# A chunked recurrence whose ten-step inverse is spread over two rounds instead of one

## The chip, the core and the metric

The kernel runs on one core of a Trainium2 chip. The metric is the device time of one execution in microseconds. The core has five engines, each of which executes its own instructions in their order and waits for others by semaphores: TensorE (PE, matrix products, output to the PSUM memory), VectorE (DVE) and ScalarE (ACT, both elementwise), GpSimd (POOL) and SyncE (SP, which here issues the DMA transfers).

## The reference

Two layers over 512 latent and 256 context tokens of width 1024. Each layer mixes tokens by attention and by a gated recurrence (RWKV-7), projects, and then runs a product-key expert layer (PEER). Only the recurrence is touched. Per head (8 heads of 64, two directions) it is a scan over the tokens:

```python
def step(state, inp):
    r_t, w_t, k_t, v_t, kk_t, b_t = inp
    s_kk = jnp.einsum('bhij,bhj->bhi', state, kk_t)
    state = state * w_t[:, :, None, :] - s_kk[..., None] * b_t[:, :, None, :] + v_t[..., None] * k_t[:, :, None, :]
    y = jnp.einsum('bhij,bhj->bhi', state, r_t) if emit else None
    return state, y
...
for d in range(N_DIRS):
    reverse = d == 1
    s_ctx, y_ctx = rwkv_direction(feats_ctx, d, s0, reverse, need_ctx_out)
    _, y_lat = rwkv_direction(feats_lat, d, s_ctx, reverse, True)
```

The latent scan starts from the state in which the context scan ended. In the last layer the context outputs are not wanted.

## The kernel before

The function `rwkv` runs once per layer. It cuts the scan into 12 chunks of 64 tokens, 4 of context and 8 of latents, with all 8 heads and both directions of a chunk side by side in one set of tiles. Inside a chunk the steps are done as matrix products, which needs the inverse of a 64 by 64 triangular matrix for each head and direction. Only the state `H` passes from chunk to chunk. The work on a chunk is cut into stages; each is a list of small functions:

- `load`: twelve DMAs, all issued by SP, bring the chunk's features: eight into `fal` (L755), four into `fbl` (L757). Both tiles have two buffers, so the load for a chunk waits until the chunk two before it has been read.
- stage_a: `Ex` and `En`, exponentials of the decays, on ScalarE (L768, L769), from `fbl`; then on VectorE `etot`, `KR` (L777, L779), `bh` and `kh` (L783, L784), and on ScalarE `vz`.
- stage_b: products of `KR` with `bh` and `kh`. `dm` (L797) is the first of their results on VectorE, followed by `AT`, `BG`, `GK` (L804 to L813); then transposed copies `kn`, `BG`, `Vb` on ScalarE.
- stage_c: the inverse of the 8 by 8 blocks on the diagonal, some thirty small VectorE instructions (D8 L837, Nb L843, the X chain L848 to L852) up to the first `W` (L856).
- stage_d: ten steps that make the whole inverse of it, each needing the one before: three times [`WT`: transpose on TensorE (the flip, L736) and copy on ScalarE (L740); `S`: product W·AT on TensorE and subtraction on VectorE (L873); `W`: product S·WT and copy on ScalarE (L879)], and last `XB`: product BG·W and copy on ScalarE (L886).
- stage_e: with the state of the chunk before, `Zs` (L910), the new `H` (L926 to L929) and the outputs (`Yc`, `Yl`, L947 to L949). `outputs` normalises and gates finished pairs of chunks (L983 to L1015).

The loop at the end of `rwkv` weaves the stages of neighbouring chunks into rounds. In round m stand stage_e of chunk m-2, all of stage_d of chunk m-1, stage_b and stage_c of chunk m, stage_a of chunk m+1, the load of chunk m+2 and the outputs of chunk m-3. `merge` sorts the functions by the positions given (from 0 to 1 within a round); after it a scheduler fixes the order on each engine, which the program then keeps. Products go to a pool of three PSUM buffers, named `wk`. All products of a round are on TensorE in one order (L717, L730, L736 are the helpers that issue them).

Of the kernel before, what the change touches and what calls it, by code (L numbers as in the profile page):

```python
# [101 lines left out]
def body(ctx: ExitStack, tc: tile.TileContext, I: dict, out: bass.AP):  # L102
# [588 lines left out]
    def rwkv(L, PT, cat, FD, need_ctx, ro, rl):  # L691
# [15 lines left out]
        def t8(nm, n, w=64):  # L707
            return ra.tile([128, 4, 2, w], F32, name=nm, bufs=n).rearrange("p g s n -> p s g n")
# [37 lines left out]
        def stage_a(s):  # L746
            def load():
                NCH, n = TOK[s["st"]] // C, s["n"]
                fal = s["fal"] = rl.tile([128, 3, 2, 4, C], F32, name="fal", bufs=2)
                fbl = s["fbl"] = rl.tile([128, 3, 2, 4, C], F32, name="fbl", bufs=2)  # L750
                for hf in range(2):
                    fd = FD[s["st"], hf]
                    for pp in range(2):
                        for d in range(2):
                            SP.dma_start(fal[:, :, pp, 2 * hf + d, :],  # L755
                                         fd["a"][NCH - 1 - n if d else n, pp].rearrange("p (f t) -> p f t", t=C))
                        SP.dma_start(fbl[:, :, pp, 2 * hf:2 * hf + 2, :],  # L757
                                     fd["b"][n, pp].rearrange("p (f d t) -> p f d t", d=2, t=C))

            def dv(f, d):  # L760
                t = s["fal"][:, f, :, d::2, :]
                return t[:, :, :, ::-1] if d else t

            def a1():
                Ex = s["Ex"] = t8("Ex", 2, 65)
                En = s["En"] = t8("En", 2)
                V.memset(Ex[:, :, :, 0:1], 1.0)
                A.activation(Ex[:, :, :, 1:65], s["fbl"][:, 2], AF.Exp, scale=-EXPC)  # L768
                A.activation(En, s["fbl"][:, 2], AF.Exp, scale=EXPC)  # L769
                s["etot"] = t8("etot", 5, 1)  # L770
                V.tensor_copy(s["etot"], Ex[:, :, :, 64:65])

            def a2(d):
                if d == 0:
                    s["KR"] = t8("KR", 4, 128)
                KR, Ex = s["KR"], s["Ex"]
                V.tensor_tensor(KR[:, :, d::2, 0:64], dv(1, d), Ex[:, :, d::2, 0:64], op=mul)  # L777
                if s["emit"]:
                    V.tensor_tensor(KR[:, :, d::2, 64:128], dv(0, d), Ex[:, :, d::2, 1:65], op=mul)  # L779

            def a3():
                s["kh"], s["bh"], s["vz"] = t8("kh", 2), t8("bh", 2), t8("vz", 2)
                V.tensor_tensor(s["bh"], s["fbl"][:, 1], s["En"], op=mul)  # L783
                V.tensor_tensor(s["kh"], s["fbl"][:, 0], s["En"], op=mul)  # L784
                for d in range(2):
                    A.copy(s["vz"][:, :, d::2, :], dv(2, d))

            return [load], [a1, lambda: a2(0), lambda: a2(1), a3]

        def stage_b(s):  # L790
            w = 128 if s["emit"] else 64

            def b0():
                gt = quad(work(), 64)
                cross(gt, s["KR"][:, :, :, 0:64], s["bh"])
                dm = s["dm"] = t8("dm", 1)
                V.tensor_tensor(dm, gt, bc(K("n8")), op=mul)  # L797

            def b1():
                gb = quad(work(), w)  # L800
                cross(gb, s["bh"], s["KR"][:, :, :, :w])
                s["AT"] = t8("AT", 3)
                BG = s["BG"] = t8("BG", 3, 128)
                V.tensor_tensor(s["AT"], gb[:, :, :, 0:64], bc(K("mp")), op=mul)  # L804
                if s["emit"]:
                    V.tensor_tensor(BG[:, :, :, 64:128], gb[:, :, :, 64:128], bc(K("n")[:, 64:128]), op=mul)
                V.tensor_tensor(s["AT"], s["AT"], bc(K("eye")), op=add)

            def b2():
                gk = quad(work(), w)  # L810
                cross(gk, s["kh"], s["KR"][:, :, :, :w])
                s["GK"] = t8("GK", 3, 128)
                V.tensor_tensor(s["GK"][:, :, :, :w], gk,  # L813
                                K("m")[:, None, None, :w].to_broadcast([128, 2, 4, w]), op=mul)

            def b3():
                t = work()
                flips(t[:, 0, :], s["kh"])
                flips(t[:, 1, :], s["bh"])
                s["kn"] = t8("kn", 3)  # L820
                unflip(s["kn"], t[:, 0, :])
                unflip(s["BG"][:, :, :, 0:64], t[:, 1, :], -0.5)

            def b4():
                t = work()
                flips(t[:, 0, :], s["vz"])
                s["Vb"] = t8("Vb", 3)
                unflip(s["Vb"], t[:, 0, :])

            return [b0, b1, b2, b3, b4]  # L830

        def stage_c(s):
            w = {}

            def c0():
                w["D"] = ra.tile([128, 8, 8], F32, name="D8", bufs=2)
                V.tensor_reduce(w["D"], flat(s["dm"]).rearrange("p x (b j) -> p x j b", j=8), axis=AX.X, op=add)  # L837

            def c2(q0):
                if q0 == 1:  # L840
                    w["N"] = ra.tile([128, 8, 8, 8], F32, name="Nb")
                for q in range(q0, min(8, q0 + 4)):
                    V.stream_shuffle(w["N"][:, q], w["D"], [(x // 8) * 8 + q for x in range(32)])  # L843

            def c3(q):
                if q == 7:
                    w["X"] = ra.tile([128, 8, 8], F32, name="X8", bufs=2)
                    V.tensor_copy(w["X"], K("eye8")[:, None, :].to_broadcast([128, 8, 8]))  # L848
                tm = ra.tile([128, 8, 8], F32, name="xtm", bufs=2)
                X8, Nb = w["X"], w["N"]  # L850
                V.tensor_tensor(tm[:, :, :q], X8[:, :, q:q + 1].to_broadcast([128, 8, q]), Nb[:, q, :, :q], op=mul)
                V.tensor_tensor(X8[:, :, :q], X8[:, :, :q], tm[:, :, :q], op=add)  # L852

            def c4():
                W = s["W"] = t8("W", 4)
                V.tensor_tensor(flat(W).rearrange("p x (b t) -> p x b t", t=8),  # L856
                                w["X"][:, :, None, :].to_broadcast([128, 8, 8, 8]),
                                K("x8")[:, None, :, None].to_broadcast([128, 8, 8, 8]), op=mul)

            return [c0, lambda: c2(1), lambda: c2(5)] + [lambda q=q: c3(q) for q in range(7, 0, -1)] + [c4]  # L860

        def stage_d(s):
            def d0():
                t = work()
                flips(t[:, 0, :], s["W"])
                s["WT"] = t8("WT", 2)
                unflip(s["WT"], t[:, 0, :])

            def d1():
                t = quad(work(), 64)  # L870
                cross(t, s["AT"], s["W"])
                s["S"] = t8("S", 2)
                V.tensor_tensor(s["S"], bc(K("eye2")), t, op=sub)  # L873

            def d2():
                t = quad(work(), 64)
                cross(t, s["WT"], s["S"])
                s["W"] = t8("W", 4)
                A.copy(s["W"], t)  # L879

            def d3():
                w = 128 if s["emit"] else 64
                t = quad(work(), w)
                cross(t, s["W"], s["BG"][:, :, :, :w])
                s["XB"] = t8("XB", 2, 128)
                A.copy(s["XB"][:, :, :, :w], t)  # L886

            return [d0, d1, d2] * 3 + [d3]
# [137 lines left out]
        NI = len(items)  # L1026
        for f in AA[0][0] + AA[0][1] + AA[1][0]:
            f()
        for st in ("c", "l")[0 if need_ctx else 1:]:
            gate_in(st)  # L1030
        for m in range(NI + 2):
            todo = []
            if m >= 2:
                todo.append((0.0, 0.8, stage_e(SS[m - 2])))
            if 1 <= m <= NI:
                todo.append((0.02, 1.0, stage_d(SS[m - 1])))
            if m < NI:
                todo.append((0.0, 0.4, stage_b(SS[m])))
                todo.append((0.15, 1.0, stage_c(SS[m])))
            if m >= 3:  # L1040
                st, n = items[m - 3]
                if (st == "l" or need_ctx) and n >= TOK[st] // C // 2:
                    todo.append((0.0, 0.9, outputs(st, n, bank)))
            if m + 2 < NI:
                todo.append((0.0, 0.1, AA[m + 2][0]))
            if m + 1 < NI:
                todo.append((0.55, 1.0, AA[m + 1][1]))
            merge(*todo)
# [729 lines left out]
```

## Time and profile before

| | us |
|---|---|
| median of 3 runs (lowest, highest) | 4801.51 (4800.45, 4802.5) |
| profiled execution, own time | 4804.7 |
| its span, first to last instruction | 4802.9 |
| TensorE busy, share of the span | 4308.1, 90% |
| VectorE busy | 3620.7, 75% |
| ScalarE busy | 1942.4, 40% |
| mean granted TensorE clock | 0.953 |

The span is taken by the hardware profiler and is 1.8 us shorter than that execution's time. Times of instructions are counted from the span's start. The recurrence of layer 0 runs from about 463 to 778 us, that of layer 1 from about 3125 to 3418 us. Shares over the whole span say little of them: most of it is the projections and the expert layers.

### The profile page before, as it was taken

Reading aid. Unit: us, or ns where it says so; the run is one execution under the profiler, and the core shown is the slowest. Engines: PE = TensorE matmul, PEld = TensorE weight load, DVE = VectorE, ACT = ScalarE, POOL = GpSimd, SP = SyncE. Lnnn points to the kernel's source line nnn. Section 1 sums busy time; section 2 is a strip of 40 time slices with the busy share of each in tenths; the row PEclk is TensorE's granted clock in tenths of the full one; section 3 lists DMA queues with packets and bytes.
Section 4 is the critical chain, followed back from the end, with each engine's and each line's share of the span. In section 5 each row is a group of like instructions: output and inputs, shape, how many; then the busy total and the mean of one; then the engine's idle time right before and its main releaser. Section 6 shows DMA issues by size and latency. Waiting matters only on the chain. (4 is left out here: it accounts for less than half of the span.)

```text
span 4802.9 us, 85326 instructions
## 1 busy us (share of the span) xinstructions
PE 4308.1 (90%) x32715; PEld 3589.6 (75%) x32715; DVE 3620.7 (75%) x7842; ACT 1942.4 (40%) x3407; POOL 1353.9 (28%) x1256
## 2 busy tenths in 40 slices
PE   7998688886999999988899989867898999999999
PEld 5664576765787887767787778456777997899998
DVE  3457665899997888877788656766579977878885
ACT  3355333435675222222222234633336763333332
POOL 0201001442222345545455231200122102244441
PEclk8999899998999999999999999979999999999999
DMA  6656314535678999988889632751334769999995
GB/s 239 243 174 197 79 51 151 184 118 180 233 267 315 349 323 332 321 292 301 294 324 321 225 126 80 207 133 43 106 132 168 257 237 334 346 330 337 331 329 208
DMA packets 576904, 1106.71 MB, mean 230 GB/s; under 512 B 145328, under 2 KB 358000, under 8 KB 566768
## 3 DMA queue, kind: packets, MB, share of 16 engines
q1 hardware_dynamic: 465904, 698.56, 42.6%
q0 software_dynamic: 110592, 402.70, 23.4%
q8 instruction: 257, 4.21, 0.4%
q14 instruction: 151, 1.24, 0.1%
HBM read 960.37 MB, written 140.74 MB: 229 GB/s over the span
## 5 line engine op out<-in xcount | busy, mean ns | idle before, releaser
L158 PE MATMUL u_ps<-phi,uhi 128*128 128x512 f32 (+1 forms) x2048 | 766.7, 374 | 62.3 <-ACT ga L1473 45.5
L1282 POOL DMA_INDIRECT u<-in_u,eidx x384 | 480.6, 1252 | 1171.6 <-DVE u L1294 833.9
L158 PE MATMUL u_ps<-phi,ulo 128*128 128x512 f32 (+1 forms) x2048 | 757.8, 370 | 35.7 <-DVE ulo L1468 35.5
L158 PE MATMUL u_ps<-plo,uhi 128*128 128x512 f32 (+1 forms) x2048 | 754.8, 369 | 0.0
L1282 POOL DMA_INDIRECT u<-in_v,eidx x384 | 516.1, 1344 | 516.9 <-DVE gacc L1307 437.1
L1467 ACT CAST uhi<-raw 128x1024 fp32r<-128x1024 f32 x256 | 268.4, 1049 | 910.7 <-PE u_ps L158 564.5
L158 PE MATMUL pa<-vhi,whi 128*128 128x512 f32 x1536 | 601.4, 392 | 9.8 <-ACT whi L149 9.8
L158 PE MATMUL pa<-vlo,whi 128*128 128x512 f32 x1536 | 601.0, 391 | 0.0
L158 PE MATMUL pa<-vhi,wlo 128*128 128x512 f32 x1536 | 600.5, 391 | 0.0
L1294 DVE SCALAR_TENSOR_TENSOR u<-u,gh 128x1024 f32<-128x1024 f32 x384 | 469.0, 1231 | 122.7 <-DMA u<-in_u,eidx 113.5
L1307 DVE SCALAR_TENSOR_TENSOR gacc<-u,gw,gacc 128x1024 f32<-128x1024 f32 x381 | 488.2, 1281 | 92.6 <-DMA u<-in_v,eidx 89.4
L158 PEld LDWEIGHTS u_ps<-phi,uhi 128*128 128x128 f32 x2048 | 392.7, 192 | 117.3 <-ACT ga L1473 55.3
L158 PEld LDWEIGHTS u_ps<-phi,ulo 128*128 128x128 f32 x2048 | 392.1, 191 | 83.2 <-DVE ulo L1468 40.5
L158 PEld LDWEIGHTS u_ps<-plo,uhi 128*128 128x128 f32 x2048 | 392.9, 192 | 44.5
L1468 DVE TENSOR_TENSOR ulo<-raw,uhi 128x1024 fp32r<-128x1024 f32 x256 | 312.9, 1222 | 136.3 <-ACT uhi L1467 134.5
L149 ACT CAST whi<-w 128x512 fp32r<-128x512 f32 (+1 forms) x256 | 145.1, 567 | 629.5 <-DVE w L1615 383.3
L158 PEld LDWEIGHTS pa<-vhi,whi 128*128 128x128 f32 x1536 | 290.2, 189 | 69.0 <-issue 10.1
L158 PEld LDWEIGHTS pa<-vhi,wlo 128*128 128x128 f32 x1536 | 289.8, 189 | 61.5
L158 PEld LDWEIGHTS pa<-vlo,whi 128*128 128x128 f32 x1536 | 290.1, 189 | 58.6
L1601 DVE TENSOR_TENSOR vlo<-vraw,vhi 128x1024 fp32r<-128x1024 f32 x256 | 312.2, 1220 | 25.8 <-ACT vhi L1600 25.7
L1600 ACT CAST vhi<-vraw 128x1024 fp32r<-128x1024 f32 x256 | 263.5, 1048 | 57.7 <-PE pa L158 35.2
L1552 DVE TENSOR_SCALAR oh<-cst,gT 128x128 f32<-128x128 f32 x896 | 253.2, 351 | 0.0
(867 smaller groups left out, 8619.1 us busy)
## 6 DMA issues: line engine op xcount, KB each, us to landing
raw<-in_ut SPq DMA_DIRECT2D x256, 512.0 KB
vraw<-in_v SPq DMA_DIRECT2D x256, 512.0 KB
gscr<-Gs SPq DMA_DIRECT2D x28, 2048.0 KB
mod_w<-in_mod_w SPq DMA_DIRECT2D x48, 1024.0 KB
Gt<-gscr SPq DMA_DIRECT2D x32, 1024.0 KB
raw<-in_w_q SPq DMA_DIRECT2D x48, 512.0 KB
Gt<-gscr SPq DMA_DIRECT2D x32, 768.0 KB
wo<-in_w_out SPq DMA_DIRECT2D x40, 512.0 KB
```

The lines of the kernel that those rows point to most:

```text
L149: A.copy(hi, src)
L158: PE.matmul(ps, a, b, start=first and q == 0 and j == 0, stop=last and q == n - 1 and j == 2)
L1282: G.indirect_dma_start(out=t, out_offset=None, in_=I[f"{tab}{l}"], in_offset=bass.IndirectOffsetOnAxis(ap=res["e"][:, e:e + 1], axis=0))
L1294: V.scalar_tensor_tensor(u, u, 1.0, c["h"], op0=mul, op1=mul, accum_out=c["act"][:, e:e + 1])
L1307: V.scalar_tensor_tensor(acc, v, w[:, e:e + 1], acc, op0=mul, op1=add)
L1467: A.copy(uhi, ut)
L1468: ins = V.tensor_tensor(ulo, ut, uhi.bitcast(F32), op=sub)
L1552: V.tensor_scalar(o2[:, t, :], io, T3[:, 1, t0 + t:t0 + t + 1], T3[:, 2, t0 + t:t0 + t + 1], op0=ALU.is_equal, op1=mul)
L1600: A.copy(r["vhi"], vt)
L1601: gafter(V.tensor_tensor(r["vlo"], vt, r["vhi"].bitcast(F32), op=sub), f)
```

## The change

The ten steps of stage_d are cut in two lists of five: `DD[m - 1][:5]` (WT, S, W, WT, S) of a chunk runs in the round in which all ten ran before; `DD[m - 2][5:]` (W, WT, S, W, XB) runs a round later, beside the first five of the next chunk. stage_e and the outputs come one round later too, so the loop has one round more. Tiles that now live longer get more buffers (etot 6, KR 5, AT, BG, GK, kn and Vb 4, W 6). stage_b is spread over 0.6 of a round instead of 0.4. The number of instructions that compute is the same. The edits of `GK`, `kn`, `Vb` and the second `W` have the form of those shown.

```diff
@@ -767,12 +767,12 @@
...
-                s["etot"] = t8("etot", 5, 1)
+                s["etot"] = t8("etot", 6, 1)
...
-                    s["KR"] = t8("KR", 4, 128)
+                    s["KR"] = t8("KR", 5, 128)
...
@@ -799,8 +799,8 @@
...
-                s["AT"] = t8("AT", 3)
-                BG = s["BG"] = t8("BG", 3, 128)
+                s["AT"] = t8("AT", 4)
+                BG = s["BG"] = t8("BG", 4, 128)
...
@@ -852,7 +852,7 @@
...
-                W = s["W"] = t8("W", 4)
+                W = s["W"] = t8("W", 6)
...
@@ -1028,17 +1028,20 @@
             f()
         for st in ("c", "l")[0 if need_ctx else 1:]:
             gate_in(st)
-        for m in range(NI + 2):
+        DD = [stage_d(s) for s in SS]
+        for m in range(NI + 3):
             todo = []
-            if m >= 2:
-                todo.append((0.0, 0.8, stage_e(SS[m - 2])))
+            if m >= 3:
+                todo.append((0.0, 0.9, stage_e(SS[m - 3])))
+            if 2 <= m < NI + 2:
+                todo.append((0.02, 1.0, DD[m - 2][5:]))
             if 1 <= m <= NI:
-                todo.append((0.02, 1.0, stage_d(SS[m - 1])))
+                todo.append((0.1, 1.0, DD[m - 1][:5]))
             if m < NI:
-                todo.append((0.0, 0.4, stage_b(SS[m])))
+                todo.append((0.0, 0.6, stage_b(SS[m])))
                 todo.append((0.15, 1.0, stage_c(SS[m])))
-            if m >= 3:
-                st, n = items[m - 3]
+            if m >= 4:
+                st, n = items[m - 4]
                 if (st == "l" or need_ctx) and n >= TOK[st] // C // 2:
                     todo.append((0.0, 0.9, outputs(st, n, bank)))
             if m + 2 < NI:
```

On ScalarE, in the round of layer 0 that ends at `dm` of chunk 5, this stands around `Ex` of chunk 8 before (names are tiles and their numbers, `out<-in`):

```order
L722 COPY settle_6017<-wk_6000 128x8
L768 ACTIVATE Ex_7447<-fbl_6688 128x2x4x64
L769 ACTIVATE En_7448<-fbl_6688 128x2x4x64
L879 COPY W_6063<-wk_6046 128x2x4x64
L740 ACTIVATE WT_6102<-wk_6097 128x512
L879 COPY W_6169<-wk_6152 128x2x4x64
L886 COPY XB_6198<-wk_6181 128x2x4x128
```

and this after the change:

```order
L786 COPY vz_6413<-fal_5568 128x2x2x64 x2
L879 COPY W_5855<-wk_5838 128x2x4x64
L768 ACTIVATE Ex_7208<-fbl_6421 128x2x4x64
L769 ACTIVATE En_7209<-fbl_6421 128x2x4x64
L879 COPY W_5906<-wk_5889 128x2x4x64
L740 ACTIVATE WT_5919<-wk_5914 128x512
L947 COPY Yc_5497<-zy_5601 128x2x2x64 x2
L886 COPY XB_5964<-wk_5947 128x2x4x128
```

Before, the two `W` copies, a `WT` and the `XB` behind `Ex` all belong to one chunk. After, the `W` copy ahead of `Ex` and the `WT` belong to one chunk, the `W` and the `XB` behind it to the chunk before that.

On TensorE, the same round, up to the product `bh`·`KR` from which `dm` is made, before (cst with W is the flip):

```order
L730 MATMUL zy_5816<-XB_5772,Zs_5945 64x64 x13
L736 MATMUL wk_6097<-cst_60,W_6063 128x128 x4
L717 MATMUL wk_6128<-W_6063,AT_5442 64x64 x16
L717 MATMUL zy_6242<-GK_5485,Vb_5565 64x64 x13
L717 MATMUL wk_6152<-S_6145,WT_6102 64x64 x16
L717 MATMUL zy_6242<-GK_5485,Vb_5565 64x64 x3
L717 MATMUL zy_6242<-Vb_5565,GK_5485 64x64 x8
L717 MATMUL wk_6181<-BG_5443,W_6169 64x128 x16
L717 MATMUL wk_6202<-bh_6175,KR_6104 64x64 x16
```

and after:

```order
L717 MATMUL wk_5889<-S_5829,WT_5749 64x64 x16
L736 MATMUL wk_5914<-cst_60,W_5855 128x128 x4
L730 MATMUL zy_5601<-XB_5538,Zs_5723 64x64 x16
L717 MATMUL wk_5947<-BG_4945,W_5906 64x128 x16
L717 MATMUL wk_5966<-W_5855,AT_5278 64x64 x16
L717 MATMUL wk_6008<-bh_5986,KR_5908 64x64 x16
```

The flip (of W_5855) and the state's products (zy from XB and Zs) now stand ahead of the product BG·W, the steps S·WT and W·AT between them are gone.

On SyncE, a load in layer 1 (chunk 7), before:

```order
L757 DMA fbl_30589<-fdb1l1_26020 128x3x128
L757 DMA fbl_30965<-fdb1l0_26018 128x3x128 x2
L757 DMA fbl_30965<-fdb1l1_26020 128x3x128
L755 DMA fal_30964<-fda1l0_26017 128x3x64 x4
L755 DMA fal_30964<-fda1l1_26019 128x3x64 x4
L757 DMA fbl_30965<-fdb1l1_26020 128x3x128
```

and after:

```order
L757 DMA fbl_30788<-fdb1l0_26018 128x3x128 x2
L757 DMA fbl_30788<-fdb1l1_26020 128x3x128 x2
L755 DMA fal_30787<-fda1l0_26017 128x3x64 x4
L755 DMA fal_30787<-fda1l1_26019 128x3x64 x4
L757 DMA fbl_31164<-fdb1l0_26018 128x3x128 x2
```

The fourth `fbl` transfer has moved from behind the eight `fal` transfers to the front. (The first row of before is of chunk 6, the last of after of chunk 8.)

On VectorE, at the start of layer 0, `bh` and `kh` of chunk 3 stood behind `etot` and the first `KR` of chunk 4, and so behind its `Ex`; after the change they stand ahead of them.

## Rows read from the trace of the kernel before

**Rows 1.** The page, chain that ended last: share of the span by engine

```profile
PE 22%; DVE 2%; DMA 0%; issue 0%; ACT 0%; POOL 0%; DVEq 0%; SPq 0%
```

**Rows 2.** Busy time by stretch: length, each engine, granted clock, DMA share, GB/s

```profile
562.67:589.31 26.64, 18.61 (x569) 16.68 (x569) 15.71 (x51) 8.36 (x18) 0.00 (x0) 0.87 0.25 62
709.83:728.02 18.19, 16.19 (x569) 14.64 (x569) 12.94 (x43) 6.76 (x14) 0.00 (x0) 1.00 0.02 4
577.00:582.40 5.40, 0.08 (x2) 0.00 (x0) 1.50 (x5) 1.62 (x3) 0.00 (x0) 0.89 0.73 183
582.40:588.00 5.60, 5.45 (x128) 4.77 (x132) 1.49 (x3) 1.18 (x2) 0.00 (x0) 0.50 0.33 74
```

**Rows 3.** VectorE in order of time, dm: start, duration, idle before and releaser

```profile
537.05 0.69 DVE L797 TENSOR_TENSOR dm<-wk,cst 128x512 f32<-128x512 f32 x1 [8.88 <-PE wk L717]
...
562.67 0.69 DVE L797 TENSOR_TENSOR dm<-wk,cst 128x512 f32<-128x512 f32 x1 [2.77 <-PE wk L717]
...
589.31 0.69 DVE L797 TENSOR_TENSOR dm<-wk,cst 128x512 f32<-128x512 f32 x1 [3.12 <-PE wk L717]
...
670.98 0.69 DVE L797 TENSOR_TENSOR dm<-wk,cst 128x512 f32<-128x512 f32 x1 [3.35 <-PE wk L717]
...
728.02 0.69 DVE L797 TENSOR_TENSOR dm<-wk,cst 128x512 f32<-128x512 f32 x1 [2.57 <-PE wk L717]
...
3188.88 0.69 DVE L797 TENSOR_TENSOR dm<-wk,cst 128x512 f32<-128x512 f32 x1 [6.18 <-PE wk L717]
...
3210.93 0.69 DVE L797 TENSOR_TENSOR dm<-wk,cst 128x512 f32<-128x512 f32 x1 [5.41 <-PE wk L717]
...
3310.83 0.69 DVE L797 TENSOR_TENSOR dm<-wk,cst 128x512 f32<-128x512 f32 x1 [2.78 <-PE wk L717]
...
3367.70 0.69 DVE L797 TENSOR_TENSOR dm<-wk,cst 128x512 f32<-128x512 f32 x1 [2.57 <-PE wk L717]
```

**Rows 4.** End of the VectorE block at 574 us, and the load behind it

```profile
574.01 0.68 DVE L783 TENSOR_TENSOR bh<-fbl,En 128x512 f32<-128x512 f32 x1
...
574.73 3.55 SPq L757 DMA_DIRECT2D fbl<-fdb0l  x4
```

**Rows 5.** ScalarE in the round from 562.67

```profile
580.75 0.63 ACT L768 ACTIVATE Ex<-fbl 128x512 f32<-128x512 f32 x1 [7.48 <-DMA fbl<-fdb0l]
...
581.81 0.57 ACT L879 COPY W<-wk 128x512 f32<-128x512 f32 x1
```

**Rows 6.** TensorE in the same round

```profile
582.43 1.11 PE L736 MATMUL wk<-cst,W 128*128 128x128 f32 x4 [5.35 <-ACT W L879]
...
587.34 1.43 PE L717 MATMUL wk<-BG,W 64*64 64x128 f32 x32
588.60 0.63 PE L717 MATMUL wk<-bh,KR 64*64 64x64 f32 x32
```

**Rows 7.** Layer 1, from Ex to dm at 3188.88: ScalarE, then TensorE

```profile
3185.67 0.63 ACT L768 ACTIVATE Ex<-fbl 128x512 f32<-128x512 f32 x1 [7.03 <-DMA fbl<-fdb1l]
...
3186.83 1.13 PE L717 MATMUL wk<-BG,W 64*64 64x64 f32 x32 [6.44 <-ACT W L879]
3187.73 1.08 PE L717 MATMUL wk<-bh,KR 64*64 64x64 f32 x32
```

**Rows 8.** ScalarE, Ex of chunk 5 in either layer

```profile
511.16 0.64 ACT L768 ACTIVATE Ex<-fbl 128x512 f32<-128x512 f32 x1 [4.87 <-DMA fbl<-fdb0l]
...
3165.68 0.64 ACT L768 ACTIVATE Ex<-fbl 128x512 f32<-128x512 f32 x1 [0.26 <-DMA bt<-bon_l]
```

**Rows 9.** Layer 1, a load: end of bh, the eight fal issues, Ex

```profile
3195.64 0.69 DVE L783 TENSOR_TENSOR bh<-fbl,En 128x512 f32<-128x512 f32 x1
...
3198.30 6.07 SPq L755 DMA_DIRECT2D fal<-fda1l  x8
...
3207.72 0.63 ACT L768 ACTIVATE Ex<-fbl 128x512 f32<-128x512 f32 x1 [5.64 <-DMA fbl<-fdb1l]
```

More of the change, by code (lines that the diff above doesn't have):

```diff
@@ L811, in b2 @@
                 cross(gk, s["kh"], s["KR"][:, :, :, :w])
-                s["GK"] = t8("GK", 3, 128)
+                s["GK"] = t8("GK", 4, 128)
                 V.tensor_tensor(s["GK"][:, :, :, :w], gk,
@@ L819, in b3 @@
                 flips(t[:, 1, :], s["bh"])
-                s["kn"] = t8("kn", 3)
+                s["kn"] = t8("kn", 4)
                 unflip(s["kn"], t[:, 0, :])
@@ L826, in b4 @@
                 flips(t[:, 0, :], s["vz"])
-                s["Vb"] = t8("Vb", 3)
+                s["Vb"] = t8("Vb", 4)
                 unflip(s["Vb"], t[:, 0, :])
@@ L877, in d2 @@
                 cross(t, s["WT"], s["S"])
-                s["W"] = t8("W", 4)
+                s["W"] = t8("W", 6)
                 A.copy(s["W"], t)
```

## The prediction

> **What bounds the kernel now.** I read the chain of waits first: it lies on TensorE [rows 1] in the last PEER pass, far behind the two stretches that the change touches, so it says nothing about them. The instruction order says that outside the two recurrences (and a few rows right behind each) nothing moves. What a recurrence gains or loses is therefore passed on whole to what follows it. So I read the two recurrences alone: by stretch, then instruction by instruction on VectorE, ScalarE, SyncE's queue and TensorE around one round.
>
> A round is counted from one `dm` to the next; dm_k is that of chunk k. In layer 0 dm_4 to dm_8 takes 108.31 us, four rounds of 27.08; these are the rounds in which the features of a later chunk are loaded. dm_8 to dm_11, without loads, takes 57.04, three rounds of 19.01 [rows 3]. The difference is a cycle through the load. Take dm_4 to dm_5, 26.64 us:
> - VectorE works without a break from `dm` at 562.67 to the end of `bh` (574.01 + 0.68), 12.0 us [rows 3, 4]. Reading `bh` frees the buffer `fbl` for the chunk two further on, and 0.04 us later SyncE issues that load [rows 4].
> - The load lands, and `Ex` starts at 580.75, 6.06 us after `bh`; ScalarE sat idle for 7.48 us with nothing but that DMA to wait for [rows 5].
> - Ready work is queued behind `Ex` on ScalarE: the `W` copy at 581.81 belongs to the inverse of another chunk [rows 5]. TensorE, idle for 5.35 us, waits for it [rows 6]. Then five of the ten serial steps (flip, S, product, copy, `BG`·W) run off before `bh`·KR at 588.60 and dm_5 at 589.31: 8.56 us from `Ex` [rows 3, 6].
>
> 12.0 + 6.06 + 8.56 = 26.62. TensorE is busy for 18.61 of these 26.64 us, in the unloaded round for 16.19 of 18.19 [rows 2].
>
> **Steady rounds.** The number of loads, products and copies stays; the reader should follow only what stands between `Ex` and `dm`. In the new order only this is left behind `Ex`: `En`, one `W` copy, `BG`·W, one W·AT with its S, `bh`·KR. The flip of the other chunk's W and the last products of stage_e stand before, where they run during the load wait. Priced by rows: `Ex`, `En` and the copy take 1.63 (580.75 to 581.81 is two starts, the copy 0.57 more) [rows 5]. `bh`·KR and W·AT are the same form: 0.63 each at the full clock, 1.08 at half [rows 6, 7]. `BG`·W is twice as wide: 1.43 in this round, where the clock was rising again [rows 6]; at the two levels I estimate 1.1 and 2.1, by twice the narrow form with some overlap. S and the waits between engines add some 0.3 to 0.6. Together 4.3 to 5.9 us. The nearest row is layer 1's round at 3185.67, where the order already had just copy, `BG`·W and `bh`·KR behind `Ex`: dm_3 starts 3.21 after it, at half clock [rows 3, 7]; with `En` (0.53), W·AT (0.9) and a `BG`·W twice as wide (0.9) that is 5.5. I take 5.2.
>
> The other two pieces: the load's 6.06 stays, since the same instruction frees the same buffer. VectorE's block from `dm` to `bh` holds the same instructions, except that the small X chain now runs uninterrupted, so that its dependent steps have nothing between them; I add 0.5 (0 to 1). New round: 12.5 + 6.05 + 5.2 = 23.75 against 26.64, −2.9 (bounds −1.5 to −4.2; the lower one if output work of the context chunks delays `bh`). Four rounds: −11.6.
>
> Rounds without a load have no wait to skip. TensorE leaves 2.0 idle of 18.19 [rows 2], which bounds the gain; I take −0.6 each, three: −1.8 (0 to −6).
>
> **The first rounds.** Here most comes from which load a `dm` stands behind. Before, dm_3 runs after `Ex` of chunk 6: all ten steps of a chunk lie in one round, and the copies that it needs stand behind that `Ex` on ScalarE. In the new order dm_3 stands behind `Ex` of chunk 5 only. That one ran at 511.16 [rows 8] and is not later now, as the `bh` that frees its buffer now stands before `Ex` of chunk 4 instead of behind it. Between it and dm_3 VectorE has some 8 us: seven instructions of the size of `bh` (0.6 from start to start), four of half that, a dozen small ones (an estimate). So dm_3 at 519 or a little earlier against 537.05, −18; I take −19. From there dm_4 is one new round away (12.5 + 6.05 + 5.2): 541.8 against 562.67, −21. I take −22, as the 8 us may well be less (bounds −17 and −26, with that block at 12 and at 4).
>
> Layer 1: `Ex` of chunk 5 at 3165.68 [rows 8], dm_3 then at 3173.7 to 3175 against 3188.88 [rows 3]. To dm_4 there is a second gain: before, SyncE issues three quarters of `fbl`, then eight of `fal`, and only then the last quarter on which `Ex` waits, so `Ex` follows the end of `bh` (3195.64 + 0.69) by 11.4 us, with the eight issues taking 6.07 of it [rows 9]. In the new order all four quarters come first, and the load costs 6.05 as in layer 0. Against that, 1.4 more behind `Ex` (4.6 for 3.21), and `Ex` of chunk 6 still has to be done by then. I take −16 for dm_4 (bounds −11 to −20). dm_4 to dm_8 takes 99.9 before [rows 3]; after, three rounds of 23.75, and one of 21.5 with a shorter VectorE block (in the round at 3188.88 it was 6.8 to the start of `bh` instead of 11.3 [rows 3, 9]): 92.75, −7.2 (−4 to −11). Unloaded rounds −1.5 (0 to −5).
>
> **The end.** There is one more round per layer, but the last chunk's ten steps still follow dm_11 one after the other as before, with less other work beside them. I cost it at nothing; what hides it is that the added round does in its first half what the old one did in its second. Without that cover it costs up to a round, 19.0 [rows 3], per layer; at best it saves 4. The larger buffers add no instruction.
>
> **Sum.** Layer 0: −22 − 11.6 − 1.8 = −35.4. Layer 1: −16 − 7.2 − 1.5 = −24.7. Together −60. The profiled execution took 4804.7, so 4744.7; it lies 3.2 above the median of the runs (4801.51), which puts the median at 4741.5; I say 4742.
>
> **The clock.** In the wait from 577 to 582.4 TensorE is nearly idle, and behind it, from 582.4 to 588, the granted clock is 0.50, 1.2 GHz [rows 2]. The Trainium skill, "TensorE: Matmul & The Clock Gate", section "HAM oscillation — how this bites in real kernels", has a kernel in which every tile's DMA wait sends the clock to half, again and again. The trace agrees. By that rule the wait that stays would put the new short path at half clock in every round, 5.9 instead of 5.2: 6 us more over eight rounds, 4748. If the products that now stand in the wait hold the clock, it is 4.3 and 4735. The sum above does not rest on it.
>
> **Rivals.**
> - The fill gains, the steady rounds don't. VectorE's in-order block before `bh` now has S and AT of two chunks in it; if it waits there for TensorE (18.6 busy in what would be 23.75 us) as much as `Ex`-to-`dm` got shorter, `bh` and the load slip and the round stays at 26.6. For it: TensorE would be busy for 78 per cent of the round. Against: before, VectorE runs through this block without a wait. −22 − 16: 4804.7 − 38 − 3.2 = 4763.
> - No change: the fill's −19 and −15 are repaid by a full added round of 19 at each end, and the steady rounds stay: about 4801. Against: both would have to hold.
> - Slower: the `W` copies still queue behind `Ex` and both halves need one, so that dm in each round waits for the second of them too; `Ex` to `dm` stays at 8.5 or more, no round shortens, the fill needs two loads as before, and the added round is paid in full, 2 × 19.0: 4840. It decides from the point where the two recurrences gain less than 19 us each. Against: the order has one copy between `Ex` and `BG`·W.
> - More: the short path at 4.3 in all eight loaded rounds (−7), dm_4 at its best bound in both layers (−4 and −4), and 4 us saved at each end (−8): −83, 4719.
>
> **Chances.** Forecast 0.60 (its own range 4730 to 4755), fills only 0.16, more 0.12, no change 0.05, slower 0.07. The range reaches to the two neighbours: 4716 to 4780. A measurement of this kernel can tell about 0.2%, 9.6 us. Faster 0.87, within that 0.05, slower 0.08.
>
> **What would show it.** Right: in layer 0 `Ex` to `dm` of 4.3 to 5.9 us where it was 8.56, loaded rounds near 23.8, dm_4 some 22 us earlier after the start of the recurrence, and in layer 1 all four `fbl` issues right behind `bh`. Wrong: idle time of VectorE before `S` or `AT` inside the block from `dm` to `bh`; `Ex` no longer waiting for its DMA but dm waiting for TensorE; a second round as long as 19 us behind dm_11 beside those that were there before.

## The result and the profile after

The changed kernel takes 4748.68 us (median of 4 runs, 4743.33 to 4753.17) against 4800.98 (4 runs, 4800.39 to 4802.5): a ratio of 0.9888, with a 95% interval of 0.9874 to 0.9901. Faster, then, by 52 us. The forecast was 4742, its range 4716 to 4780.

| | before | after |
|---|---|---|
| profiled execution, own time | 4804.7 | 4753.17 |
| its span | 4802.9 | 4751.4 |
| TensorE busy | 4308.1 | 4288.6 |
| mean granted TensorE clock | 0.953 | 0.957 |

First the frame: where the `dm` of the first chunk starts in either layer, VectorE of the kernel before (start, duration, and in brackets the idle time before it with what ended it),

```profile
470.82 0.68 DVE L797 TENSOR_TENSOR dm<-wk,cst 128x512 f32<-128x512 f32 x1
...
3127.48 0.69 DVE L797 TENSOR_TENSOR dm<-wk,cst 128x512 f32<-128x512 f32 x1 [0.78 <-PE wk L717]
```

and in the kernel after: dm_0, dm_4, dm_5, dm_6, dm_11 of layer 0, then dm_0, dm_4, dm_8, dm_11 of layer 1, the answers to [rows 3]:

```profile
471.88 0.69 DVE L797 TENSOR_TENSOR dm<-wk,cst 128x512 f32<-128x512 f32 x1
...
542.81 0.69 DVE L797 TENSOR_TENSOR dm<-wk,cst 128x512 f32<-128x512 f32 x1 [0.17 <-PE wk L717]
...
566.78 0.69 DVE L797 TENSOR_TENSOR dm<-wk,cst 128x512 f32<-128x512 f32 x1 [0.16 <-PE wk L717]
...
591.23 0.69 DVE L797 TENSOR_TENSOR dm<-wk,cst 128x512 f32<-128x512 f32 x1 [0.17 <-PE wk L717]
...
691.91 0.68 DVE L797 TENSOR_TENSOR dm<-wk,cst 128x512 f32<-128x512 f32 x1
...
3101.05 0.69 DVE L797 TENSOR_TENSOR dm<-wk,cst 128x512 f32<-128x512 f32 x1 [0.77 <-PE wk L717]
...
3162.85 0.69 DVE L797 TENSOR_TENSOR dm<-wk,cst 128x512 f32<-128x512 f32 x1
...
3248.62 0.68 DVE L797 TENSOR_TENSOR dm<-wk,cst 128x512 f32<-128x512 f32 x1
...
3302.80 0.69 DVE L797 TENSOR_TENSOR dm<-wk,cst 128x512 f32<-128x512 f32 x1
```

A recurrence hands over to the rest of its layer at the first product of the output projection. These are TensorE's rows of it, layer 0 and layer 1, before,

```profile
787.93 1.86 PE L158 MATMUL acc_ps<-wohi,chi 128*128 128x512 f32 x4
...
3425.45 2.07 PE L158 MATMUL acc_ps<-wohi,chi 128*128 128x512 f32 x4 [1.31 <-ACT wohi L149]
```

and after:

```profile
764.62 1.20 PE L158 MATMUL acc_ps<-wohi,chi 128*128 128x512 f32 x2
...
3375.51 0.77 PE L158 MATMUL acc_ps<-wohi,chi 128*128 128x512 f32 x1
```

The differences of these rows and of [rows 3] are the whole account (us; dm_8 of layer 0 after is at 638.48):

| stretch | before | after | change | forecast |
|---|---|---|---|---|
| layer 0, dm_0 to dm_4 | 91.85 | 70.93 | −20.9 | −22 |
| dm_4 to dm_8, four loaded rounds | 108.31 | 95.67 | −12.6 | −11.6 |
| dm_8 to dm_11 | 57.04 | 53.43 | −3.6 | −1.8 |
| dm_11 to the projection | 59.91 | 72.71 | +12.8 | 0 |
| layer 1, dm_0 to dm_4 | 83.45 | 61.80 | −21.7 | −16 |
| dm_4 to dm_8 | 99.90 | 85.77 | −14.1 | −7.2 |
| dm_8 to dm_11 | 56.87 | 54.18 | −2.7 | −1.5 |
| dm_11 to the projection | 57.75 | 72.71 | +15.0 | 0 |
| all that lies outside | | | −3.6 | 0 |

They add up to −51.4; the spans differ by 51.5. The recurrences gain 75.6, more than forecast, and their ends give 27.8 back, which was not forecast.

Now one loaded round, dm_5 to dm_6 of layer 0, as [rows 4 to 6] showed one before (dm_4 to dm_5): VectorE, SyncE's queue, ScalarE, TensorE.

```profile
578.42 0.69 DVE L783 TENSOR_TENSOR bh<-fbl,En 128x512 f32<-128x512 f32 x1
...
579.13 2.52 SPq L757 DMA_DIRECT2D fbl<-fdb0l  x4
...
580.52 0.59 ACT L879 COPY W<-wk 128x512 f32<-128x512 f32 x1
585.80 0.64 ACT L768 ACTIVATE Ex<-fbl 128x512 f32<-128x512 f32 x1 [4.70 <-DMA fbl<-fdb0l]
586.35 0.61 ACT L769 ACTIVATE En<-fbl 128x512 f32<-128x512 f32 x1
586.86 0.57 ACT L879 COPY W<-wk 128x512 f32<-128x512 f32 x1
...
587.48 1.98 PE L717 MATMUL wk<-BG,W 64*64 64x128 f32 x32 [4.21 <-ACT W L879]
589.24 1.08 PE L717 MATMUL wk<-W,AT 64*64 64x64 f32 x32
590.09 1.08 PE L717 MATMUL wk<-bh,KR 64*64 64x64 f32 x32
```

The first `W` copy has got in front of `Ex`; only the second still waits behind it. From `dm` to the end of `bh` 12.33 us, to `Ex` 6.69, to the next `dm` 5.43: together 24.45, where the round before took 12.0 + 6.06 + 8.56. The wait for the load is still there; what is queued behind it got shorter.

In layer 1 the load that follows dm_5 (3182.25) answers [rows 9]: the end of VectorE's block, SyncE's queue, `Ex`.

```profile
3192.68 0.69 DVE L783 TENSOR_TENSOR bh<-fbl,En 128x512 f32<-128x512 f32 x1
...
3193.39 3.00 SPq L757 DMA_DIRECT2D fbl<-fdb1l  x4
3196.49 5.21 SPq L755 DMA_DIRECT2D fal<-fda1l  x8
...
3199.09 0.64 ACT L768 ACTIVATE Ex<-fbl 128x512 f32<-128x512 f32 x1 [3.64 <-DMA fbl<-fdb1l]
```

All four `fbl` transfers now go ahead of the eight `fal`, and `Ex` follows the end of `bh` by 5.72 us, before by 11.4. dm_6 is at 3203.66, 4.57 behind `Ex`.

The windows of the kernel after (length; busy time and count of PE, PEld, which loads PE's weights, DVE, ACT and POOL; granted clock, DMA share, GB/s): the round of layer 0 shown above, the half clock behind its wait, a layer 1 stretch behind such a wait, and the end of layer 0.

```profile
566.78:591.23 24.45, 18.52 (x580) 16.68 (x576) 15.87 (x51) 8.71 (x17) 0.00 (x0) 0.85 0.27 68
585.80:591.20 5.40, 3.72 (x108) 3.72 (x112) 0.69 (x1) 3.14 (x5) 0.00 (x0) 0.50 0.43 98
3221.30:3225.70 4.40, 2.74 (x110) 2.74 (x113) 0.73 (x2) 3.12 (x5) 0.00 (x0) 0.82 0.56 128
691.91:764.62 72.71, 61.18 (x1611) 52.53 (x1600) 35.44 (x87) 24.31 (x43) 10.37 (x7) 0.90 0.17 50
```

The end of layer 0 before:

```profile
728.02:787.93 59.91, 49.65 (x1208) 41.70 (x1208) 28.79 (x78) 19.15 (x35) 8.72 (x6) 0.93 0.18 51
```

TensorE is busy for 61.18 of 72.71 us after dm_11, before for 49.65 of 59.91: the stretch is 12.8 us longer, and TensorE has 11.5 us more to do in it, with a third more matmuls (1611 to 1208). In layer 1 it is 60.54 of 72.71 to 48.94 of 57.75. In layer 0 nearly all of it comes from the front: from dm_0 to dm_4 TensorE ran 1553 matmuls before (54.53 us) and runs 1160 now (43.68 us).

### The profile page after: what moved, and what is told of

The parts are those of the page before. It is cut to its first block, busy times and chain, and to the rows that moved or that the text cites. A ratio compares the mean times of both kernels' runs of the same rounds, so it can differ in the third digit from the quotient of the medians.

```text
span 4751.4 us, 85354 instructions
## 1 busy us (share of the span) xinstructions
PE 4288.6 (90%) x32715; PEld 3568.5 (75%) x32715; DVE 3619.3 (76%) x7842; ACT 1952.0 (41%) x3407; POOL 1366.7 (29%) x1256
## 3 DMA queue, kind: packets, MB, share of 16 engines
q8 instruction: 257, 4.21, 0.4%
```

## The experiments

The first theory, from the prediction (P below): rounds were long because ready copies stand on ScalarE behind an `Ex` that waits for its load. Its rival (S): they were long because the ten steps are a serial chain that doesn't fit a round, so that only the cut itself helps. Each ratio is to the kernel before, run beside it on the same chip, with a 95% interval. Chips differ, so distances to the kernel after go by the ratios. The edits are made to the kernel before or to the one after, as said.

**e1, the kernel before with a third buffer for the features** (and **e2**, the same edit on the kernel after).

```diff
-                fal = s["fal"] = rl.tile([128, 3, 2, 4, C], F32, name="fal", bufs=2)
-                fbl = s["fbl"] = rl.tile([128, 3, 2, 4, C], F32, name="fbl", bufs=2)
+                third = s["i"] % 3 == 2
+                pool, x, k = (ra, "x", 1) if third else (rl, "", 2)
+                fal = s["fal"] = pool.tile([128, 3, 2, 4, C], F32, name="fal" + x, bufs=k)
+                fbl = s["fbl"] = pool.tile([128, 3, 2, 4, C], F32, name="fbl" + x, bufs=k)
...
```

(`s["i"]` is the number of the chunk.)

> The kernel before with a third buffer for the features (every third chunk's fal and fbl in tiles of their own), steps of the inverse unsplit. My theory: the round is set by the load cycle (bh frees the buffer, load, Ex, and the steps queued behind Ex). With a third buffer the load leaves the cycle, Ex no longer waits for its DMA, and loaded rounds come down from 27 us to about those without a load, 19 to 20.5; with the first rounds that is 60 to 95 us: about 4725 (4705 to 4742). Rival A, the ten serial steps of one chunk in one round are what is too long, load or not: loaded rounds stay above 24 us, 4775 or more.

> The changed kernel with the same third buffer. My theory: the split is worth its 52 us mainly because fewer steps stand behind the load wait; without that wait it is worth only the 1.2 us a round that unloaded rounds showed, less the 7 us at each end: within -15 and +5 us of the kernel before with a third buffer, about 4720. Rival A: the split pays with or without the wait, so at least 40 us below the kernel before with a third buffer.

e1: 4759.4, ratio 0.9917 (0.9903 to 0.993): neither number. e2: 4723.63, 0.9843 (0.9829 to 0.9856), some 22 us below the kernel after; it is 36 below e1, again between the two expectations. ScalarE in a round of e1 shows why e1 falls short:

```profile
559.72 0.59 ACT L881 COPY W<-wk 128x512 f32<-128x512 f32 x1 [1.11 <-PE wk L717]
563.47 0.63 ACT L770 ACTIVATE Ex<-fblx 128x512 f32<-128x512 f32 x1 [3.16 <-DVE KR L781]
564.01 0.58 ACT L740 ACTIVATE kn<-wk 128x512 f32<-128x512 f32 x1
```

`Ex` no longer waits for its DMA, but now stands so early that it waits for VectorE to read the `Ex` buffer that it overwrites, with `kn`, `BG`, `Vb` and `WT` ready behind it. One wait took the place of the other, at the head of the same queue. So the load isn't the point by itself; what stands behind a waiting `Ex` may be, which e9 tests.

**e3, the kernel after, the last chunk's ten steps in one round as before, without the added round.**

```diff
-        for m in range(NI + 3):
+        for m in range(NI + 2):
...
+            if m == NI + 1:
+                todo.append((0.5, 1.0, stage_e(SS[m - 2])))
-            if 2 <= m < NI + 2:
+            if 2 <= m < NI + 1:
                 todo.append((0.02, 1.0, DD[m - 2][5:]))
             if 1 <= m <= NI:
-                todo.append((0.1, 1.0, DD[m - 1][:5]))
+                todo.append((0.1, 1.0, DD[m - 1][:5] if m < NI else DD[m - 1]))
```

(The `stage_e` of the chunk before and the last outputs are fitted into that round too.)

> The changed kernel, but the last chunk does all ten steps in one round and its stage_e follows in the same round as that of the chunk before, so that the loop has no extra round. My theory: the added round cost 7.7 and 6.6 us at the two ends (dm of the last chunk to the last Yl), and this gives back 8 to 18: about 4735. Rival B: the ends are set by the serial chain of the output normalisation, and the added round is not what costs: within 4 us of the changed kernel, 4745 to 4752.

4759.9, ratio 0.992 (0.9906 to 0.9934): neither number, and some 15 us slower than the kernel after. In its layer 0, dm_11 starts at 684.09 and the projection at 761.34:

```profile
684.09:761.34 77.25, 63.31 (x1610) 53.92 (x1600) 34.68 (x87) 24.25 (x43) 10.38 (x7) 0.89 0.16 47
```

The last inverse was done sooner: the last two `XB` copies run one behind the other from 37.5 us after dm_11, where the last one of the kernel after starts at 48.45. But the end grew by 4.5 us. It has as many matmuls behind dm_11 as the kernel after (1610), so what fills the end is rather this work than the added round as a row of steps. With each chunk finished a round later, half an inverse and the state and outputs of one more chunk stand behind dm_11.

**e4, the kernel before with the `fbl` transfers issued ahead of the `fal` ones.**

```diff
+                        SP.dma_start(fbl[:, :, pp, 2 * hf:2 * hf + 2, :],
+                                     fd["b"][n, pp].rearrange("p (f d t) -> p f d t", d=2, t=C))
+                for hf in range(2):
+                    fd = FD[s["st"], hf]
+                    for pp in range(2):
                         for d in range(2):
                             SP.dma_start(fal[:, :, pp, 2 * hf + d, :],
                                          fd["a"][NCH - 1 - n if d else n, pp].rearrange("p (f t) -> p f t", t=C))
-                        SP.dma_start(fbl[:, :, pp, 2 * hf:2 * hf + 2, :],
-                                     fd["b"][n, pp].rearrange("p (f d t) -> p f d t", d=2, t=C))
```

> The kernel before, only that a load issues its four fbl transfers ahead of the eight fal transfers. Rival C: layer 1 gained because the change happened to bring the last fbl quarter to the front; then this alone gives layer 1 about 5 us in each of five or six loaded rounds, and in layer 0 the first rounds a few: -25 to -35, about 4770, and the split itself is worth only the other 20 to 25. If the shorter path behind Ex made most of layer 1's gain: -5 to -15, about 4790.

4791.53, ratio 0.9981 (0.9971 to 0.999). Layer 1's dm_0 and dm_11 start at

```profile
3121.97 0.68 DVE L800 TENSOR_TENSOR dm<-wk,cst 128x512 f32<-128x512 f32 x1
...
3353.64 0.69 DVE L800 TENSOR_TENSOR dm<-wk,cst 128x512 f32<-128x512 f32 x1 [2.57 <-PE wk L717]
```

231.67 apart, before 240.22 [rows 3, with 3127.48 above]. So the order of the transfers alone, in the kernel before, is worth some 8.5 of layer 1's 38 us.

**e5, the kernel before, and e6, the kernel after, with one buffer for `Ex` and `En` instead of two.** This takes memory away; it keeps `Ex` from standing early.

```diff
-                Ex = s["Ex"] = t8("Ex", 2, 65)
-                En = s["En"] = t8("En", 2)
+                Ex = s["Ex"] = t8("Ex", 1, 65)
+                En = s["En"] = t8("En", 1)
```

> The kernel before with one buffer instead of two for Ex and En. Ex of a chunk then stands on ScalarE behind the last reader of the chunk before it, a round later, when its load has long landed; the features keep two buffers. My theory (a good part of the loaded round is a ready copy queued behind an Ex that waits for its DMA): Ex no longer waits for a DMA from chunk 5 on, loaded rounds without output work fall to 20 to 23 us as with the third feature buffer, about 4760 (4745 to 4772). Rival A (the ten steps in one round are too long, wait or not): loaded rounds stay above 25, 4785 or more.

> The changed kernel with one buffer for Ex and En. The gains of the split and of an Ex that waits for nothing were found to add up with a third feature buffer (-25 us against the changed kernel), and this does the same without it: about 4724 (4714 to 4736). If the third buffer gained by the early transfers themselves and not by what stands behind Ex: 4745 to 4755.

e5: 4758.45, ratio 0.9918 (0.9904 to 0.9931). e6: 4718.44, 0.9834 (0.982 to 0.9847), some 26 us below the kernel after. A buffer less makes both kernels faster. That speaks for P, though in layer 0 of e5 `Ex` still waits, 17.3 us in all for `KR`.

**e7, the kernel after with the cut behind the third step instead of the fifth.**

```diff
-                todo.append((0.02, 1.0, DD[m - 2][5:]))
+                todo.append((0.02, 1.0, DD[m - 2][3:]))
-                todo.append((0.1, 1.0, DD[m - 1][:5]))
+                todo.append((0.1, 1.0, DD[m - 1][:3]))
```

> The changed kernel with the ten steps cut after the third instead of the fifth. What stands behind Ex is again two copies and BG times W, with one product. Theory P (the path behind the wait is what shortened): within 8 us of the changed kernel, 4741 to 4757, Ex to dm between 4 and 6 us. Theory S (the longest stretch of serial steps in one round counts): seven steps instead of five in a round, so a third to a half of the gain is lost: 4765 to 4780, and rounds without a load go from 18.4 back towards 19.3.

4760.74, ratio 0.9918 (0.9903 to 0.9932), between the two expectations. In layer 0 `Ex` to `dm` was 3.7 to 7.8 us, and the three unloaded rounds took 58.16, longer than the 53.43 of the kernel after; at 19.4 each they fit S, which had them go back towards 19.3. Moving the cut changed both what stands behind `Ex` and the serial part of a round. It didn't tell the theories apart.

**e8, the kernel after with the second flip of `W` done six times over in chunks 2 to 6**, to keep TensorE busy in the wait.

```diff
+        WARM = range(2, 7)
...
-                flips(t[:, 0, :], s["W"])
+                s["k"] = s.get("k", 0) + 1
+                for _ in range(6 if s["k"] == 2 and s["i"] in WARM else 1):
+                    flips(t[:, 0, :], s["W"])
...
```

> The changed kernel, but in chunks 2 to 6 the flip that stands ahead of BG times W in the load wait is done six times over into the same buffer (the results are the same), which fills some 3 of the 4.2 us in which TensorE idles there. If the half clock behind the wait costs what the rows say (1.98, 1.08 and 1.08 us at half clock), a clock held at 1.00 makes Ex to dm 4.3 instead of 5.4 us in up to five rounds a layer: -3 to -11 against the changed kernel. If the repeated flips don't hold the clock, or reach beyond Ex: 0 to +10.

4748.65, ratio 0.9899 (0.9884 to 0.9915): no difference from the kernel after, where 3 to 11 us less were expected of a held clock. The clock was held, as TensorE's rows of the round show, with the fillers in the first:

```profile
577.46 2.84 PE L736 MATMUL wk<-cst,W 128*128 128x128 f32 x24
580.23 1.15 PE L730 MATMUL zy<-XB,Zs 64*64 64x64 f32 x32
584.08 1.10 PE L717 MATMUL wk<-BG,W 64*64 64x128 f32 x32 [2.71 <-ACT W L883]
585.01 0.64 PE L717 MATMUL wk<-W,AT 64*64 64x64 f32 x32
585.47 0.65 PE L717 MATMUL wk<-bh,KR 64*64 64x64 f32 x32
```

`BG`·W takes 1.10 instead of 1.98, the two behind it 0.65 instead of 1.08, and `Ex` to `dm` is 3.9 instead of 5.4 in three rounds. The two rounds that also carry output work grew, from 23.7 and 23.5 to 25.5 and 25.6. What the half clock costs in a round is 1.5 us; the fillers got it back and lost it elsewhere.

**e9, the kernel before (ten steps in one round) with `Ex` and `En` tied to the state `H` of the round**, by a bias of zero made from it. Nothing is split; only `Ex` can't stand early.

```diff
-                A.activation(Ex[:, :, :, 1:65], s["fbl"][:, 2], AF.Exp, scale=-EXPC)
-                A.activation(En, s["fbl"][:, 2], AF.Exp, scale=EXPC)
+                if H[0] is None:
...
+                else:
+                    z = ra.tile([128, 1], F32, name="zb", bufs=2)
+                    V.tensor_scalar(z, H[0][:, 0, 0, 0:1], 0.0, None, op0=mul)
+                    A.activation(Ex[:, :, :, 1:65], s["fbl"][:, 2], AF.Exp, scale=-EXPC, bias=z)
+                    A.activation(En, s["fbl"][:, 2], AF.Exp, scale=EXPC, bias=z)
```

(While there is no `H` yet, the two are as before.)

> The kernel before, unsplit, but Ex and En take as their bias a zero made from the state H of the round (one tiny VectorE instruction more per chunk), so that no Ex can stand on ScalarE ahead of its own round; nothing waits for a load. With Ex moved by its buffers alone (one buffer) Ex still waited 3 us for KR with copies behind it, and the split was then worth 40 us. Theory P (a waiting Ex with ready copies behind it makes the unsplit round long): without any such wait loaded rounds without output work come to 19.3 to 21, 4742 to 4754. Theory S (ten serial steps in a round): they stay at 22 to 23, 4756 to 4765.

4722.78 (4715.29 to 4730.93), ratio 0.9834 (0.9815 to 0.9852): some 26 us below the kernel after, with all ten steps in one round and no round added, and lower than either theory had it. ScalarE's waits in the recurrence of layer 0 (what waited for what: us in all, times, longest) before:

```profile
ACT W L879 <- PE wk L717: 44.0, 23, 4.9
ACT Ex L768 <- DMA fbl<-fdb0l: 39.5, 7, 7.5
```

after the change:

```profile
ACT Ex L768 <- DMA fbl<-fdb0l: 17.9, 6, 4.7
...
ACT W L879 <- PE wk L717: 9.9, 12, 2.3
```

and in e9:

```profile
ACT W L885 <- PE wk L717: 41.5, 30, 5.7
...
ACT Ex L774 <- DVE zb L773: 2.3, 4, 1.1
```

The wait of `Ex` for the latent loads, 39.5 us, is gone. The serial steps still show, as waits of `W` for its product. A loaded round without output work, and one with:

```profile
539.60:559.68 20.08, 16.73 (x596) 15.04 (x597) 15.82 (x54) 8.75 (x18) 0.00 (x0) 1.00 0.33 82
559.68:583.50 23.82, 20.66 (x586) 17.96 (x587) 18.47 (x61) 9.88 (x20) 2.91 (x2) 1.00 0.33 80
```

20.08 against 26.64 before and 23.97 after (542.81 to 566.78), within P's 19.3 to 21 and below S's 22 to 23. TensorE was busy in the round for 18.61 us with 569 matmuls [rows 2], here at full clock for 16.73 with 596, or 15.97 for 569: an estimate of the clock's part of these 6.6 us is at most 2.6. The order of the transfers isn't the cause either: in e9's layer 1 three `fal` transfers go ahead of the first `fbl`. In layer 0 even the first rounds get the whole gain of the cut: dm_0 to dm_4 takes 71.2 (468.37 to 539.60), with the cut 70.9, before 91.85. In layer 1 they get part of it: 68.4, with the cut 61.8, before 83.45.

**e10, the kernel after with the edit of e9.**

> The changed kernel with the same tie of Ex to the state H. Rounds of 18.4 to 20 us throughout, about 4715 (4706 to 4724). Theory P: the split is then worth only the first rounds (some 15 to 20 a layer) and 1 us in each later round, less the 7 at each end: 20 to 32 us below the unsplit kernel with the tie. Theory S: 38 or more below it.

4717.06 (4713.24 to 4727.92), ratio 0.9826 (0.9806 to 0.9846). dm_0, dm_11 and the first product of the projection in its layer 1:

```profile
3081.46 0.69 DVE L803 TENSOR_TENSOR dm<-wk,cst 128x512 f32<-128x512 f32 x1 [0.77 <-PE wk L717]
...
3270.10 0.69 DVE L803 TENSOR_TENSOR dm<-wk,cst 128x512 f32<-128x512 f32 x1 [0.32 <-PE wk L717]
...
3342.74 2.05 PE L158 MATMUL acc_ps<-wohi,chi 128*128 128x512 f32 x4
```

Both recurrences, dm_0 to dm_11 and on to the projection, by the same rows as above:

| | layer 0 | its end | layer 1 | its end | sum |
|---|---|---|---|---|---|
| before | 257.2 | 59.9 | 240.2 | 57.8 | 615.1 |
| after | 220.0 | 72.7 | 201.8 | 72.7 | 567.2 |
| e9, not cut, `Ex` late | 221.6 | 60.7 | 201.9 | 56.1 | 540.3 |
| e10, cut, `Ex` late | 205.6 | 73.2 | 188.6 | 72.6 | 540.0 |

e9 has the length of the kernel after from dm_0 to dm_11, with the short ends of the kernel before. It gets there in another way: its rounds from dm_4 to dm_8 are shorter (89.7 and 74.4, with the cut 95.7 and 85.8), those from dm_8 to dm_11 longer (60.7 and 59.1, with the cut 53.4 and 54.2). In e10 the cut shortens the recurrences by 29.3 us and gives 29.0 back at the ends: nothing is left. The spans of these two executions differ by 13.9 us, but nearly all of that lies outside these stretches (from the projection of layer 0 to dm_0 of layer 1, 2346.5 in e9 and 2332.8 in e10); the medians differ by 6, and the profiled execution of e9 was the longest of its five. The intervals of e9 and e10 overlap. Neither theory's number for e10 (20 to 32 below e9, or 38 and more) came true; that the cut still helps once `Ex` is late is not shown.

**e11, the kernel before with the larger buffers alone** (etot 6, KR 5, AT, BG, GK, kn and Vb 4, W 6).

> The kernel before with only the larger buffer counts of the change (etot, KR, AT, BG, GK, kn, Vb, W). Every theory: the order of the instructions is the same but for a few products of zy, so no change, 4795 to 4806. A gain over 10 us would mean that the split needed no second list.

4803.23, ratio 1.0005 (0.9993 to 1.0016): nothing, as forecast.

## Why the prediction was right, and where not

**`Ex` to `dm`**: forecast 5.2 for 8.56 in layer 0, measured 4.4 to 5.4 in five loaded rounds. Right, for the reason given: the `W` copy and the flip went in front of the waiting `Ex`. e9 shows the mechanism from the other side, by taking the wait away and leaving the steps together.

**Steady rounds, layer 0**: 23.75 forecast, 23.92 measured (95.67 / 4). The parts differ slightly (12.33 + 6.69 + 5.43 in the round shown, for 12.5 + 6.05 + 5.2): the load took 0.6 longer than before.

**First rounds, layer 0**: −22 forecast, −20.9 measured. e9 reaches the same without the cut, where dm_3 stands behind `Ex` of chunk 3 (514.46); so "which load a `dm` stands behind" was the right reading. The sum came near by luck, though: dm_3, at 515.78, was 22.3 nearer to dm_0 than before (forecast 19), and the round from it to dm_4 took 27.03 (forecast 23.75).

**Layer 1**: −24.7 forecast, −38.5 measured, mis-sized in every term. I had carried layer 0's round over. The round from 3182.25 takes instead 11.1 to the end of `bh` (forecast 12.5), 5.7 for the load and 4.6 from `Ex` to `dm` (5.2), and the four rounds average 21.44 (85.77 / 4). e4 gives the front order of `fbl` 8.5 of it, part of which the forecast had in; why a round of layer 1 is shorter in all three parts stays open.

**The end: the step that failed.** "I cost it at nothing; what hides it is that the added round does in its first half what the old one did in its second." It cost 12.8 and 15.0. The cover that I named was one of serial steps; but the two windows of the end show TensorE busy for over four fifths of it, before and after, so its work there had to be counted, not its steps. A chunk finished a round later leaves 400 more matmuls behind dm_11, 11.5 us of TensorE. In layer 0 nearly as many, 393, are missing from dm_0 to dm_4, where TensorE had time to spare: e9 ran 1524 there in the same 71 us, the kernel after 1160. So the cut moved work out of a stretch with idle time into one that TensorE fills by over four fifths. e3 removed the round and kept the work, and the end got no shorter. The bound in the prediction (up to a round, 19.0) did hold.

The two errors, −14 in layer 1 and +28 at the ends, and 1.8 in the unloaded rounds of layer 0, cancel in part, which is luck: the time came out at 7 above the forecast.

**The rivals.** "Fills only" fell: the loaded rounds shortened by 12.6 and 14.1, and VectorE ran its block in 12.33 instead of 12.0. "No change" and "slower" fell: the ends cost 12.8 and 15.0 of the 19.0 that they priced, but both recurrences gained 37 and more. "More" was right on the recurrences and wrong on the ends.

**The clock.** Behind the wait of layer 0's round the granted clock is 0.50 (585.8 to 591.2), 1.2 GHz, with `BG`·W at 1.98. In layer 1 it is 0.82 over 3221.3 to 3225.7, where TensorE had idled for 3.32 us and `BG`·W still took 1.10. The Trainium skill, "TensorE: Matmul & The Clock Gate", section "HAM oscillation — how this bites in real kernels", tells of a kernel whose clock falls again at every wait for a DMA. The trace agrees for layer 0, and for layer 1 only in part. e8 doesn't price the term for the whole kernel: the held clock took 1.5 us off `Ex` to `dm` in three rounds, but the fillers that held it made others longer.

**What stays open.** Whether the cut is worth anything beside a late `Ex` (6 us between the medians, within the scatter, and nothing in the two recurrences with their ends). How the ends could keep their old length with the cut: e3 didn't achieve it, and no run takes the work out of the ends, so that it is the work which sets their length is argued from the counts. And which part of the change does it: e11 rules out the buffers alone, but no run has the wider spread of stage_b and the other new positions without the cut.

## What to carry to other kernels

Where an engine works in order, look at what stands behind an instruction that waits for a transfer, rather than at the wait: tying `Ex` to an event late in the round gave 79 us (4801.36 to 4722.78, runs of one chip) for a 128x1 instruction per chunk, against 52 for the cut with its larger buffers. More buffers or earlier loads don't replace this, since the instruction may then be placed earlier still and wait for something else (e1). And when a pipeline gets one stage deeper, count how much work of the busiest engine now stands behind the last input, and not how many steps.

## What was not expected of the hardware

An exponential of 128x512 takes 0.73 us with the bias from a tile, 0.64 without (ScalarE in e9; without is the changed kernel's row at 585.80 above):

```profile
578.31 0.73 ACT L774 ACTIVATE Ex<-fbl,zb 128x512 f32<-128x512 f32 x1 [1.06 <-DVE zb L773]
```

The Trainium skill, "ScalarE: Activation LUTs", section "What ACT_TABLE_LOAD costs", gives some 93 ns more for a bias that is read from a [128,1] tile; the trace agrees, with 0.09 us.

With the flips repeated, the granted clock stayed at 1.00 through the wait of e8 (577.4 to 588), where without them it was 0.50 behind the wait; TensorE then idled for 2.71 us ahead of `BG`·W instead of 4.21. With no long wait left, the clock of e9 was 1.00 in both rounds shown.
